# One layer of a hybrid SSD decoder: when weight sums are transferred, when u tiles are loaded, where the exponentials stand, and how many outputs share an accumulator

## The chip, the cores and the metric

The kernel runs on one core of a Trainium2 chip. The metric is the device time of one execution in microseconds, as the median of several runs. The engines are called PE (matmul), DVE, ACT, POOL and SP, as the profile calls them. Each takes its instructions in the order in which the program lists them. DMAs issued on POOL (software queue), SP and ACT (hardware queues) run on the same 16 DMA engines.

## What is computed

One layer of a decoder on 512 tokens and 16 learned leading tokens (528 columns), D = 1024, float32 in and out:

```python
u = rmsnorm(h, mix_norm_w)
proj = u @ w_in                                  # pool | z | xBC | dt | gates
gates = sigmoid(proj[..., OFF_GATE:] + b_gate)
y_pool = pool_mixer(u_pool, ...) @ w_pool_up     # causal means over 2, 4, 8, 16 tokens
xbc = silu(causal_depthwise_conv(xbc, conv_w, conv_b))
y = ssd_chunked(xs, softplus(dt_raw + dt_bias), -exp(a_log), B, C) + xs * d_skip
y = rmsnorm_per_group(y * silu(z)) * ssd_norm_w
h = h + (gate_pool * y_pool + gate_ssd * (y @ w_ssd_out)) @ w_o
h = h + relu(rmsnorm(h) @ w_ff1) ** 2 @ w_ff2
out = rmsnorm(h)[:, 16:]
```

The SSD part has 8 groups of 4 heads (head size 64, state 128) and runs in chunks of 128 tokens. Inside a chunk each head needs exp(a_cs[l] - a_cs[s]) below the diagonal, and exp(a_cs[l]) for what earlier chunks leave behind.

## The kernel before

Tiles have 128 partitions. A float32 operand is split into a rounded high part and the rest (`hi`, `lo`, type fp32r), and a product is three matmuls: hi x hi, hi x lo, lo x hi. A weight block (128 x 1024, 512 KB) is loaded by SP into `raw` (3 buffers), cast to `whi` by ACT (L95) and subtracted to `wlo` by DVE (L97); there are 4 buffers of each of the two.

The order of the work is made by a scheduler from the order in which the code lists it. `tc.issue_after(x)` puts what stands under it behind instruction x. Tile pools add the waits for buffers.

After a start (norm, dt, first group's projections, four gates) the program walks through the 8 groups (loop at L904). For group g, `weave` (L704) alternates the steps of these generators:

- `ssd(g)` (L569): POOL loads `abc`, the row a_cs broadcast to all partitions (L577, 1 MB, one buffer). PE transposes B and x (`ptb`, `ptm`, `ptx`). ACT makes exp(a_cs) in `eb` (L609), and the decay in `abc`: relu of the difference for two heads (L614; DVE does the other two, L617), then two exponentials (L620, L621). PE makes `pcb`, and DVE multiplies it into `abc` (L652, `masked`). PE makes the states (`pst`), the part of the earlier chunks (`po`) and of the own chunk (`py`, L667). DVE puts `yt` together (L670 to L674). ACT squares it (L679, `squared`), PE sums the squares (`png`, L685), ACT takes the root (L688), and ACT and DVE split the result (`yh`, `yl`).
- `group_proj(g + 1)` (L508): the next group's projections. B, C (and x up to group 3) are plain products (`px`, L197, L199) with a convolution (`conv`, L415: ACT L418, DVE L421, ACT's silu L423). From group 4 on, x's two tiles are made together by `pair` (L472) from seven products of sums of weights and sums of u (`pqx`, L485). Then z's two tiles (`pz`) and their silu (`zt`, L562), in some groups a gate ahead of them (`pgp`). In group 4 `out_half` (L800) comes first, in group 7 `out_part`.
- `sums_of_u` (L863) in groups 0 to 2: it loads u's tiles k and k + 4 from HBM into `ra` and `rb` (one buffer each), combines their halves on DVE (`combine`, L874), and splits the two results into the tiles `T` (`form`, L881; ACT and DVE). Group 0 does tile pair 0, group 1 does 1, group 2 does 2 and 3.
- `weight_sums_at` (L763): sums of weight blocks made by DMAs from HBM to HBM, on POOL's queue. A set takes 4 or 8 transfers, half of them with an add. Each transfer is tied to a small POOL copy (L770) of one column of `mark[0]`, the tile written last, so POOL waits for that tile; transfers are spread evenly over the steps of a group.

`out_half` (L800) makes 8 output blocks of 512 columns (`pso`) in 4 PSUM tiles of 1024 columns (`psum2`, two buffers), two blocks to a tile; ACT copies each block to SBUF (L806) and sends it to HBM.

The exponentials of `eb` (L608, L609) stand behind x's silu (`x_ready`) in groups 0 to 4 and behind z's silu (`z_ready`) in groups 5 to 7. ACT has its functions in tables: exponential, silu, sigmoid and root each need a table load (`ACT_TABLE_LOAD`) when another was used before.

The rest of the program (pool branch, merge, w_o, the MLP) follows the groups.

Of the kernel before, what the change touches and what calls it, by code (L numbers as in the profile page):

```python
# [12 lines left out]
ALU = mybir.AluOpType  # L13
# [42 lines left out]
SETS_POOL = 0  # L56

PLAIN = 4

# [5 lines left out]
def kernel(ctx: ExitStack, tc, xT, x, w, fx, f1, f2, vec, fnw, out):  # L65
# [125 lines left out]
    def proj(outs, wblk, rhs):  # L191

        for part in range(2):
            for k in range(NK):
                wt = wblk[part][:, k * P : (k + 1) * P]
                for o, c in outs:
                    pe.matmul(o, wt, rhs[0][k][:, c], start=part == 0 and k == 0, stop=part == 1 and k == NK - 1)  # L197
                    if part == 0:
                        mm[0] = pe.matmul(o, wt, rhs[1][k][:, c], start=False, stop=False)  # L199
# [10 lines left out]
    def narrow(ps):  # L210
        return [(ps, slice(NM, L))]
# [198 lines left out]


    mark = [None]
    x_ready, z_ready, filled = {}, {}, {}

    def conv(dst, src, ct):  # L415
        n = dst.shape[-1]
        e = src.shape[-1] - n
        act.activation(dst, src[:, e:], AF.Identity, bias=col(V_CB, ct), scale=col(V_CW, ct * 4 + 3))  # L418
        for j in range(1, 4):
            o = max(0, j - e)  # L420
            dve.scalar_tensor_tensor(dst[:, o:], src[:, e + o - j : e + n - j],  # L421
                                     col(V_CW, ct * 4 + 3 - j), dst[:, o:], op0=ALU.mult, op1=ALU.add)
        silu = act.activation(dst, dst, AF.Silu)  # L423
        mark[0] = dst[:, :1]
        if ct < 16:
            x_ready[ct // 2] = silu

    def group_tiles(g):
        xc = gc.tile([P, 2, L], F32, tag="xc", name=f"xc{g}")
# [42 lines left out]
    def pair(kind, g, r):  # L472

        ps = psum2(f"pq{kind}{g}")
        banks = (ps[:, :HALF], ps[:, 512 : 512 + HALF])
        operands = pair_operands(PAIRS.index((kind, g)))
        one, two = HF
        for m, f, n, start, stop in MULTIPLY:
            o = banks[n]
            wt = next(operands)  # L480
            f = factor_u(f)
            for low in range(2):
                for k in range(4):
                    wk = wt[low][:, k * P : (k + 1) * P]
                    pe.matmul(o, wk, f[k][0], start=start and not low and k == 0,  # L485
                              stop=stop and low == 1 and k == 3, skip_group_check=True)
# [21 lines left out]
    def group_proj(g, cur, gate=None):  # L508
# [60 lines left out]
    def ssd(g, cur):  # L569
# [35 lines left out]
        ap = abc.rearrange("p (i j) l -> p i j l", j=2)  # L605
        for j in range(2):
            js = slice(64 * j, 64 * j + 64)
            with tc.issue_after((z_ready if g in X_PAIRS[1:] else x_ready)[g].ins):  # L608
                act.activation(eb[js, :, :], ap[js, :, j, :], AF.Exp)  # L609
        dm = abc.rearrange("p r (c l) -> p r c l", c=4)  # L610
        for r in range(R):
# [92 lines left out]
    def weave(a, b, n, sums, side):  # L704

        end = object()
        a, sums = [a], [sums]
        while a or b or side:
            for t in [a] + [b] * n:
                for q in (t, sums):  # L710
                    if q and next(q[0], end) is end:
                        q.pop(0)
            side = [q for q in side if next(q, end) is not end]
        for q in sums:
            for _ in q:
                pass
# [23 lines left out]
            for t in sets for n in SUMS[t[0]]}  # L740

    def weight_steps():
        t = sets.pop(0)
        src = {"fx": fx, "f1": f1, "f2": f2}[t[0]][t[1]]
        o = {n: wsum[(*t, n)] for n in SUMS[t[0]]}
        put = nc.gpsimd.dma_start
        yield put(o["t1"], src[B11])
        yield put(o["s3"], src[B12])
        yield put(o["t1"], src[B12], accum_op=ALU.add)
        if "t2" in o:  # L750
            yield put(o["t2"], src[B22])
        yield put(o["s3"], src[B22], accum_op=ALU.add)
        if "t2" in o:
            yield put(o["t2"], o["t1"], accum_op=ALU.add)
            yield put(o["t4"], src[B21])
            yield put(o["t4"], o["t2"], accum_op=ALU.add)

    def weight_sums():
        for end in weight_steps():
            pass  # L760
        return end

    def weight_sums_at(n, pieces):  # L763
        total = sum(2 * len(SUMS[t[0]]) for t in sets[:n])
        steps = (e for _ in range(n) for e in weight_steps())
        put = i = 0
        while put < total:
            i += 1
            if put * pieces < i * total:
                at = pool.tensor_copy(seen, mark[0])  # L770
                with tc.issue_after(at.ins):
                    next(steps)
                put += 1
            yield
        assert next(steps, None) is None

    cur = group_tiles(0)
    for _ in group_proj(0, cur):
# [20 lines left out]

    def out_half():  # L800
        for dd in range(4):
            ps = psum2(f"pso{dd}")
            for i in range(2):
                ssd_out(2 * dd + i, ps[:, i * SEQ : (i + 1) * SEQ], range(8))
                o = staged(f"so{2 * dd + i}")
                act.copy(o, ps[:, i * SEQ : (i + 1) * SEQ])  # L806
                nc.scalar.dma_start(acc_d[2 * dd + i], o)
                mark[0] = o[:, :1]
                yield
# [50 lines left out]

    def sums_of_u(ks, g):  # L863

        one, two = HF

        def load(k):
            a, b = raw_pair("u", k)
            with tc.issue_after(abc_load[g].ins):
                for t, kk in ((a, k), (b, k + 4)):  # L870
                    nc.gpsimd.dma_start(t, u_d[kk])
            return a, b

        def combine(a, b, behind):  # L874
            with tc.issue_after(behind[g].ins):
                dve.tensor_tensor(b[:, two], a[:, two], b[:, two], op=ALU.subtract)
# [4 lines left out]
        def form(k, n, src, behind):  # L881
            hi, lo = T[n, "h", k], T[n, "l", k]
# [4 lines left out]
        t = load(ks[0])  # L887
        yield
        combine(*t, masked)
        yield  # L890
        form(ks[0], "0", t[0], y_first)
        if len(ks) > 1:
            form(ks[0], "1", t[1], y_first)
            t = load(ks[1])
        yield
        yield
        if len(ks) > 1:
            combine(*t, squared)
            form(ks[1], "0", t[0], squared)
            yield  # L900
        form(ks[-1], "1", t[1], squared)
        yield

    for g in range(G):  # L904
        nxt = group_tiles(g + 1) if g + 1 < G else None
        fill = [group_proj(g + 1, nxt, GATE_AT.get(g))] if nxt else [out_part()]
        if g == 4:
            fill = [out_half()] + fill
        weave(ssd(g, cur), fill, 2 if g == 4 else 1, weight_sums_at(SETS_AT[g], PIECES.get(g, 12)),
              [sums_of_u(SUMS_AT[g], g)] if g in SUMS_AT else [])  # L910
        cur = nxt
    gc_stack.close()
# [114 lines left out]

    for d in range(NK):
        t_load = nc.gpsimd.dma_start(acc[d], acc_d[d])
    for _ in range(SETS_POOL):  # L1030
        with tc.issue_after(t_load.ins):
            t_load = weight_sums()
    pend = [pooled_halves(*pool_tile(2 * POOL_ORDER[0] + i)) for i in range(2)]

    un = units()
# [782 lines left out]
```

## Time and profile before

| | us |
|---|---|
| median of 3 runs (1017.05 to 1018.7) | 1017.71 |
| the profiled execution | 1019.7 |
| its span, first to last instruction | 1018.0 |

The mean granted PE clock of the span is 0.996. A page of the profile gives, for one execution, the busy time of each engine and its share of the span, the span in slices, the DMA queues, the chain of work that ended last, and groups of equal instructions with their mean length and the idle time before them. Other views answer questions: a table by stretches of time, the list of who waited for whom, and the timeline of an engine. PEld is the weight load beside PE's matmuls. In a row of the timeline come start, length, engine, line, operation, output and inputs; the bracket at the end is the idle time just before it and what ended it.

### The profile page before, as it was taken

Reading aid. Unit: us, or ns where it says so; the run is one execution under the profiler, and the core shown is the slowest. Engines: PE = TensorE matmul, PEld = TensorE weight load, DVE = VectorE, ACT = ScalarE, POOL = GpSimd, SP = SyncE. Lnnn points to the kernel's source line nnn. Section 1 sums busy time; section 2 is a strip of 40 time slices with the busy share of each in tenths; the row PEclk is TensorE's granted clock in tenths of the full one; section 3 lists DMA queues with packets and bytes.
Section 4 is the critical chain, followed back from the end, with each engine's and each line's share of the span. In section 5 each row is a group of like instructions: output and inputs, shape, how many; then the busy total and the mean of one; then the engine's idle time right before and its main releaser. Section 6 shows DMA issues by size and latency. Waiting matters only on the chain.

```text
span 1018.0 us, 15702 instructions
## 1 busy us (share of the span) xinstructions
PE 998.0 (98%) x6047; PEld 876.6 (86%) x6047; DVE 799.0 (78%) x1153; ACT 603.6 (59%) x853; POOL 120.4 (12%) x215
## 2 busy tenths in 40 slices
PE   9999999999999999999999999999999999999997
PEld 7889888979788897987889888888889999999986
DVE  7968797778653787877689756877988888888885
ACT  8656769484833575665345533458656656665654
POOL 0001211212122212123400000221000000000000
PEclk9999999999999999999999999999999999999999
DMA  7265868566688748487933542879454554455432
GB/s 254 87 225 163 246 192 229 167 188 198 179 255 266 215 140 238 118 233 208 253 129 103 212 161 63 268 193 338 112 185 134 158 182 149 156 175 150 141 104 83
DMA packets 61803, 184.52 MB, mean 181 GB/s; under 512 B 7072, under 2 KB 8416, under 8 KB 60704
## 3 DMA queue, kind: packets, MB, share of 16 engines
q1 hardware_dynamic: 39456, 109.00, 32.3%
q0 software_dynamic: 18240, 67.51, 26.2%
q10 hardware_dynamic: 4032, 7.00, 1.9%
q8 instruction: 47, 0.77, 0.3%
q14 instruction: 28, 0.23, 0.1%
HBM read 173.13 MB, written 58.59 MB: 228 GB/s over the span
## 4 chain that ended last, share of the span: by engine, by line
PE 87%; ACT 6%; DMA 3%; DVE 2%; issue 1%; POOL 0%; ACTq 0%; DVEq 0%; POOLq 0%; SPq 0%
PE px L1437 8%; PE px L197 7%; PE alpha L1505 6%; PE px L1440 4%; PE px L199 4%; PE pz L197 4%; PE alpha L1508 3%; PE pgs L197 3%; PE pgp L197 2%; DMA raw<-in_w 2%; PE pqx L485 2%; PE py L667 2%; PE pz L199 2%; PE wo_alpha L1199 1%; PE pf L130 1%; PE pf L129 1%
## 5 line engine op out<-in xcount | busy, mean ns | idle before, releaser
L95 ACT CAST whi<-raw 128x1024 fp32r<-128x1024 f32 (+2 forms) x90 | 90.1, 1011 | 83.4 <-DMA raw<-in_w 18.1
L97 DVE TENSOR_TENSOR wlo<-raw,whi 128x1024 fp32r<-128x1024 f32 (+2 forms) x90 | 104.9, 1172 | 37.9 <-ACT whi L95 28.9
L197 PE MATMUL px<-uh,whi 128*128 128x264 f32 (+1 forms) x320 | 82.4, 295 | 0.0
L199 PE MATMUL px<-ul,whi 128*128 128x264 f32 (+1 forms) x320 | 79.9, 287 | 0.0
L1212 DVE TENSOR_TENSOR ht<-ht,alpha 128x1024 f32<-128x1024 f32 x35 | 42.7, 1219 | 29.1 <-PE alpha L1505 29.1
L197 PEld LDWEIGHTS px<-uh,whi 128*128 128x128 f32 x320 | 61.5, 192 | 1.3 <-issue 0.9
L199 PEld LDWEIGHTS px<-ul,whi 128*128 128x128 f32 x320 | 61.3, 192 | 0.3
L1135 ACT CAST shi<-rawf 128x1024 fp32r<-128x1024 f32 x42 | 44.2, 1053 | 28.7 <-PE alpha L1508 18.3
L1505 PE MATMUL alpha<-shi,hh 128*128 128x512 f32 x140 | 55.2, 394 | 0.0
L1508 PE MATMUL alpha<-shi,hl 128*128 128x512 f32 x140 | 54.7, 391 | 0.0
L1136 DVE TENSOR_TENSOR slo<-rawf,shi 128x1024 fp32r<-128x1024 f32 x42 | 51.2, 1218 | 0.6 <-ACT shi L1135 0.6
L1440 PE MATMUL px<-vsl,shi 128*128 128x256 f32 x192 | 47.4, 280 | 0.0
L1437 PE MATMUL px<-vsh,shi 128*128 128x256 f32 x192 | 47.4, 281 | 0.0
L197 PE MATMUL pz<-uh,whi 128*128 128x512 f32 x112 | 45.1, 402 | 1.5 <-ACT yh L697 1.3
L199 PE MATMUL pz<-ul,whi 128*128 128x512 f32 x112 | 44.6, 398 | 0.0
L197 PE MATMUL px<-uh,wlo 128*128 128x264 f32 (+1 forms) x320 | 42.5, 284 | 0.0
L197 PEld LDWEIGHTS px<-uh,wlo 128*128 128x128 f32 x320 | 40.1, 189 | 0.0
L1505 PE MATMUL alpha<-slo,hh 128*128 128x512 f32 x140 | 37.4, 389 | 0.0
L1437 PEld LDWEIGHTS px<-vsh,shi 128*128 128x128 f32 x192 | 36.2, 188 | 0.9
L1440 PEld LDWEIGHTS px<-vsl,shi 128*128 128x128 f32 x192 | 36.1, 188 | 0.9
L1440 PE MATMUL px<-vl,shi 128*128 128x256 f32 x144 | 36.1, 283 | 0.0
L1437 PE MATMUL px<-vh,shi 128*128 128x256 f32 x144 | 36.0, 282 | 0.0
(600 smaller groups left out, 3066.5 us busy)
## 6 DMA issues: line engine op xcount, KB each, us to landing
raw<-in_w SPq DMA_DIRECT2D x96, 512.0 KB, 4.9
f_t<-in_f POOLq DMA_DIRECT2D x38, 512.0 KB, 6.8
f_s<-in_f POOLq DMA_DIRECT2D x26, 512.0 KB, 7.4
b<-in_f SPq DMA_DIRECT2D x21, 512.0 KB, 4.6
rawf<-in_f SPq DMA_DIRECT2D x36, 256.0 KB, 3.0
rawf<-f_t SPq DMA_DIRECT2D x36, 256.0 KB, 2.9
abc<-acs_d POOLq DMA_DIRECT2D x8, 1024.0 KB, 7.6
f_t<-f_t POOLq DMA_DIRECT2D x12, 512.0 KB, 5.9
```

The source lines that it names most:

```text
L95: act.copy(hi[:, c], raw[:, c])
L97: dve.tensor_tensor(lo[:, c], raw[:, c], hi[:, c].bitcast(F32), op=ALU.subtract)
L197: pe.matmul(o, wt, rhs[0][k][:, c], start=part == 0 and k == 0, stop=part == 1 and k == NK - 1)
L199: mm[0] = pe.matmul(o, wt, rhs[1][k][:, c], start=False, stop=False)
L485: pe.matmul(o, wk, f[k][0], start=start and not low and k == 0, stop=stop and low == 1 and k == 3, skip_group_check=True)
L1135: splits.append((act.copy(hi, src), dve.tensor_tensor(lo, src, hi.bitcast(F32), op=ALU.subtract)))
L1136: dve.tensor_tensor(lo, src, hi.bitcast(F32), op=ALU.subtract)))
L1212: added[0] = dve.tensor_tensor(o, o, src, op=op)
L1437: pe.matmul(ps, m, f[k][0], start=start and not low and k == 0, stop=stop and low == 1 and k == 3, skip_group_check=True)
L1440: pe.matmul(ps, m, f[k][1], start=False, stop=False, skip_group_check=True)
L1505: pe.matmul(ps[t], hh[:, p, seg, st], m, start=bool(first and not low and p == 0), stop=bool(last and low and p == 1), skip_group_check=True)
L1508: pe.matmul(ps[t], hl[:, p, seg, st], m, start=False, stop=False, skip_group_check=True)
```

## The change

Five edits, in the groups alone:

- The transfers of the weight sums are given by a table (`SLOTS`): in a usual group five behind step 0, two behind step 2, one behind step 4, each bundle behind one POOL copy. Within a set (or two sets of four transfers) all plain transfers come first and the adds behind them. In `weave` the side work's step comes ahead of the sums' step.
- `sums_of_u` takes pairs 0 and 1 in group 0, 2 in group 1, 3 in group 2. A pair is asked for as soon as the pair before is split; pair 2 is so asked for in group 0, pair 3 in group 1.
- The exponentials of `eb` stand behind z's silu in all groups.
- z's products stand behind the pair's last product (`paired_up`) where there is a pair.
- Each output block of `out_half` has a PSUM tile of its own.

```diff
-SUMS_AT = {0: (0,), 1: (1,), 2: (2, 3)}
+SUMS_AT = {0: (0, 1), 1: (2,), 2: (3,)}
-SETS_AT = {0: 1, 1: 1, 2: 2, 3: 1, 4: 2, 5: 2, 6: 1, 7: 1}
-PIECES = {4: 21, 7: 14}
+SLOTS = {0: 5, 2: 2, 4: 1}
+SLOTS_LONG = {**SLOTS, 9: 4, 12: 2, 14: 2}
+SLOTS_LAST = {0: 2, 2: 2}
...
-            proj(narrow(ps), wt, X if first else U)
+            with tc.issue_after(paired_up[g].ins) if g in paired_up else nullcontext():
+                proj(narrow(ps), wt, X if first else U)
...
-            with tc.issue_after((z_ready if g in X_PAIRS[1:] else x_ready)[g].ins):
+            with tc.issue_after(z_ready[g].ins):
                 act.activation(eb[js, :, :], ap[js, :, j, :], AF.Exp)
...
-            for t in [a] + [b] * n:
-                for q in (t, sums):
-                    if q and next(q[0], end) is end:
-                        q.pop(0)
-            side = [q for q in side if next(q, end) is not end]
+            for i, t in enumerate([a] + [b] * n):
+                if t and next(t[0], end) is end:
+                    t.pop(0)
+                if i == 0:
+                    side = [q for q in side if next(q, end) is not end]
+                if sums and next(sums[0], end) is end:
+                    sums.pop(0)
...
+        for dst, src in q:
+            yield put(dst, src)
+        for dst, src in adds:
+            yield put(dst, src, accum_op=ALU.add)
...
+    def paced(slots):
+        for i in range(max(slots) + 1):
+            if i in slots:
                 at = pool.tensor_copy(seen, mark[0])
+                for _ in range(slots[i]):
+                    with tc.issue_after(at.ins):
+                        next(line)
             yield
...
         for dd in range(4):
-            ps = psum2(f"pso{dd}")
             for i in range(2):
-                ssd_out(2 * dd + i, ps[:, i * SEQ : (i + 1) * SEQ], range(8))
+                ps = psum2(f"pso{2 * dd + i}")[:, :SEQ]
+                ssd_out(2 * dd + i, ps, range(8))
...
+        if g == 0:
+            load(0)
         yield
-        combine(*t, masked)
+        combine(masked)
         yield
-        form(ks[0], "0", t[0], y_first)
-        if len(ks) > 1:
-            form(ks[0], "1", t[1], y_first)
-            t = load(ks[1])
+        form(ks[0], 0, y_first)
         yield
+        form(ks[0], 1, y_first)
+        if ks[0] < 3:
+            load(ks[0] + 1)
         yield
         if len(ks) > 1:
-            combine(*t, squared)
-            form(ks[1], "0", t[0], squared)
+            combine(squared)
             yield
-        form(ks[-1], "1", t[1], squared)
+            form(ks[1], 0, squared)
+            yield
+            form(ks[1], 1, squared)
+            load(ks[1] + 1)
         yield
```

More of the change, by code (lines that the diff above doesn't have):

```diff
@@ L484, in pair @@
                     wk = wt[low][:, k * P : (k + 1) * P]
-                    pe.matmul(o, wk, f[k][0], start=start and not low and k == 0,
-                              stop=stop and low == 1 and k == 3, skip_group_check=True)
+                    paired_up[g] = pe.matmul(o, wk, f[k][0], start=start and not low and k == 0,
+                                             stop=stop and low == 1 and k == 3, skip_group_check=True)
                     if not low:
@@ L742, in weight_steps @@
     def weight_steps():
-        t = sets.pop(0)
-        src = {"fx": fx, "f1": f1, "f2": f2}[t[0]][t[1]]
-        o = {n: wsum[(*t, n)] for n in SUMS[t[0]]}
+        ts = [sets.pop(0)]
+        if ts[0][0] == "f2" and sets and sets[0][0] == "f2":
+            ts.append(sets.pop(0))
         put = nc.gpsimd.dma_start
[L747 to L756, printed above, removed]
+        q, adds = [], []
+        for t in ts:
+            src = {"fx": fx, "f1": f1, "f2": f2}[t[0]][t[1]]
+            o = {n: wsum[(*t, n)] for n in SUMS[t[0]]}
+            q += [(o["t1"], src[B11]), (o["s3"], src[B12])]
+            adds += [(o["t1"], src[B12]), (o["s3"], src[B22])]
+            if "t2" in o:
+                q += [(o["t2"], src[B22]), (o["t4"], src[B21])]
+                adds += [(o["t2"], o["t1"]), (o["t4"], o["t2"])]
+        for dst, src in q:
+            yield put(dst, src)
+        for dst, src in adds:
+            yield put(dst, src, accum_op=ALU.add)
     def weight_sums():
@@ L761, in weight_sums @@
         return end
[L763 to L769, printed above, removed]
+    line = (e for _ in range(9) for e in weight_steps())
+    def paced(slots):
+        for i in range(max(slots) + 1):
+            if i in slots:
                 at = pool.tensor_copy(seen, mark[0])
-                with tc.issue_after(at.ins):
-                    next(steps)
-                put += 1
+                for _ in range(slots[i]):
+                    with tc.issue_after(at.ins):
+                        next(line)
             yield
-        assert next(steps, None) is None
     cur = group_tiles(0)
@@ L867, in load, with combine @@
         def load(k):
-            a, b = raw_pair("u", k)
+            raw = raw_pair("u", k)
             with tc.issue_after(abc_load[g].ins):
-                for t, kk in ((a, k), (b, k + 4)):
+                for t, kk in zip(raw, (k, k + 4)):
                     nc.gpsimd.dma_start(t, u_d[kk])
-            return a, b
-        def combine(a, b, behind):
+            u_raw.append(raw)
+        def combine(behind):
+            a, b = u_raw[-1]
             with tc.issue_after(behind[g].ins):
@@ L879, in combine, with form @@
                 dve.tensor_tensor(b[:, one], b[:, one], a[:, one], op=ALU.add)
-        def form(k, n, src, behind):
-            hi, lo = T[n, "h", k], T[n, "l", k]
+        def form(k, i, behind):
+            hi, lo = T["01"[i], "h", k], T["01"[i], "l", k]
+            src = u_raw[-1][i]
             with tc.issue_after(behind[g].ins):
@@ L908 @@
             fill = [out_half()] + fill
[L909 removed]
+        weave(ssd(g, cur), fill, 2 if g == 4 else 1, paced({4: SLOTS_LONG, 7: SLOTS_LAST}.get(g, SLOTS)),
               [sums_of_u(SUMS_AT[g], g)] if g in SUMS_AT else [])
@@ L1029 @@
         t_load = nc.gpsimd.dma_start(acc[d], acc_d[d])
-    for _ in range(SETS_POOL):
-        with tc.issue_after(t_load.ins):
-            t_load = weight_sums()
+    assert next(line, None) is None
     pend = [pooled_halves(*pool_tile(2 * POOL_ORDER[0] + i)) for i in range(2)]
```

11 lines of the change are left out of this document (4 added, 7 removed).

## The prediction

> **What bounds the kernel now.** I read the engine table first, then the chain of work that ended last, then busy time by stage, then the waits of TensorE (PE).
>
> ```profile
> PE 998.0 (98%) x6047; PEld 876.6 (86%) x6047; DVE 799.0 (78%) x1153; ACT 603.6 (59%) x853; POOL 120.4 (12%) x215
> ...
> PE 87%; ACT 6%; DMA 3%; DVE 2%; issue 1%; POOL 0%; ACTq 0%; DVEq 0%; POOLq 0%; SPq 0%
> ```
>
> PE is busy 998.0 of 1018.0 us and carries 87% of the chain. The matmuls that the change leaves are the same in number and size, so the time can fall only by PE's idle time, or by a clock that is not halved. The stages (columns: length, then PE, PEld, DVE, ACT and POOL busy with counts, PE clock, DMA share, GB/s) show where that lies:
>
> ```profile
> 115.00:160.00 45.00, 42.80 (x318) 39.53 (x318) 38.83 (x62) 33.59 (x45) 8.17 (x16) 1.00 0.74 208
> 160.00:209.00 49.00, 46.74 (x329) 42.19 (x328) 40.41 (x67) 31.90 (x43) 8.93 (x20) 0.98 0.65 186
> ...
> 265.00:357.00 92.00, 88.16 (x509) 75.50 (x509) 55.04 (x77) 48.85 (x67) 21.28 (x37) 1.00 0.80 227
> ...
> 404.00:440.00 36.00, 35.17 (x263) 33.10 (x264) 30.76 (x52) 21.80 (x34) 6.72 (x12) 0.95 0.62 176
> ...
> 496.00:1018.00 522.00, 516.53 (x2928) 453.78 (x2926) 417.70 (x549) 289.66 (x415) 25.77 (x42) 1.00 0.52 163
> ```
>
> The groups, the only place where the order changes, run from 72 to 496; PE idles there in patches (45.00 less 42.80 is 2.2 us in one, 3.8 in another). The last 522 us keep their order and are costed at nothing. In 404 to 440 the mean clock is 0.95: 0.05 x 36 is 1.8 us lost. Who made PE wait (total, times, longest):
>
> ```profile
> PE pso L129 <- ACT so L806: 2.5, 1, 2.5
> PE png L685 <- ACT qhg L311: 2.2, 2, 1.8
> PE ptx L597 <- DVE xddm L590: 1.8, 2, 1.5
> ...
> PE py L667 <- issue: 1.5, 1, 1.5
> PE pz L197 <- ACT yh L697: 1.3, 1, 1.3
> ```
>
> They are single events, seen in the timeline (start, length, engine, line, operation, and in brackets the idle time before):
>
> ```profile
> 133.24 0.99 PE L667 MATMUL py<-abc,xdt 128*64 128x128 f32 x14 [1.50 <-issue]
> 205.97 0.50 PE L685 MATMUL png<-qhg,ones_r 128*128 128x512 f32 x1 [1.77 <-ACT qhg L311]
> 208.45 0.63 PE L197 MATMUL pz<-uh,whi 128*128 128x512 f32 x1
> 211.16 0.39 PE L199 MATMUL pz<-ul,whi 128*128 128x512 f32 x1
> 280.31 0.50 PE L129 MATMUL pso<-yh,whi 128*128 128x512 f32 x1 [2.55 <-ACT so L806]
> 404.83 0.66 PE L597 MATMUL ptx<-ident,xc 128*128 128x128 f32 x4 [1.53 <-DVE xddm L590]
> ```
>
> After the idle patch at 206 a 512-column matmul takes 0.63 us in place of 0.39: the clock is halved for a while there too, as in the stage from 404. I price each halving at the 1.8 us above.
>
> **The change, part by part.**
>
> *An accumulator per output block.* Two outputs share a PSUM tile, and the second output's first matmul stands 2.55 us for the copy of the first, which is queued on ACT behind the exponentials. With a tile each, the second starts at once, and the third needs the copy only a block (24 matmuls) later. Gain 2.55.
>
> *u tiles one stage ahead.* In group 2 two tiles are loaded and the second pair is wanted in the same group:
>
> ```profile
> 193.36 0.70 POOL L871 DMA_DIRECT2D rbu<-u_d  x1
> 201.42 0.43 DVE L876 TENSOR_TENSOR rbu<-rau,rbu 128x264 f32<-128x264 f32 x1 [4.03 <-DMA rbu<-u_d]
> 203.85 0.76 DVE L421 SCALAR_TENSOR_TENSOR xc<-px,vs,xc 128x527 f32<-128x527 f32 x1
> 205.95 0.69 DVE L312 TENSOR_TENSOR qlg<-sqg,qhg 128x512 fp32r<-128x512 f32 x1
> 209.05 1.22 DVE L97 TENSOR_TENSOR wlo<-raw,whi 128x1024 fp32r<-128x1024 f32 x1
> ```
>
> DVE stands 4.03 us before it combines the pair, and qhg, png and z's products come late behind it: 1.77 plus about 0.5 in two smaller gaps, plus a halved clock. In the changed kernel groups 1 and 2 have one pair each, asked for a group earlier: gain 2.25 + 1.8.
>
> But group 0 now takes two pairs, and the second can't be asked for ahead, since the first holds its buffers. On POOL it stands behind the load of group 1's abc and behind two accumulating transfers, the second waiting until the first has landed. Rows for that:
>
> ```profile
> 97.56 0.57 POOL L577 DMA_DIRECT2D abc<-acs_d  x1 [1.41 <-PE py L667]
> 106.15 0.68 DVE L674 TENSOR_TENSOR yt<-yt,zt 128x512 f32<-128x512 f32 x1
> 112.18 1.98 PE L197 MATMUL pz<-uh,wlo 128*128 128x512 f32 x8
> ...
> fx_t<-fx_t POOLq DMA_DIRECT2D x4, 512.0 KB, 6.6
> ...
> rau<-u_d POOLq DMA_DIRECT2D x4, 264.0 KB, 8.1
> ```
>
> The first accumulation goes out shortly before abc, at about 95, and lands 6.6 us later, at 101.6; the second takes its place on the queue, and the tiles go out at about 103 and land 8.1 us later, at 111. DVE, done with y at about 105 to 106.8, stands some 5 to 6 us. Queued behind the waiting combine are two convolution steps, the group's sum of squares, its low half and the combine's next step, then the low half of z's second weight block: 0.43 + 0.76 + 0.69 + 0.76 + 0.69 + 0.43 + 1.22 = 5.0 us, so that block is ready at 116, and PE wants it at 112.18. I take 3.8 us of idle PE and one more halved clock, 1.8. Bounds: nothing if the pair lands by 107.2; 5.5 + 1.8 if it lands 1.7 later than I think. A gain is excluded, since PE doesn't wait there now.
>
> *Exponentials behind z's silu.* ACT in group 1 now:
>
> ```profile
> 114.12 1.05 ACT L95 CAST whi<-raw 128x1024 fp32r<-128x1024 f32 x1 [1.01 <-DMA raw<-in_w]
> 115.18 1.28 ACT L609 ACT_TABLE_LOAD   x1
> 116.48 1.06 ACT L609 ACTIVATE eb<-abc 64x1024 f32<-64x1024 f32 x1
> 117.55 1.28 ACT L562 ACT_TABLE_LOAD   x1
> 118.85 1.03 ACT L562 ACTIVATE zt<-pz 128x1024 f32<-128x1024 f32 x1
> ```
>
> One exponential runs ahead of silu, so its table is loaded, dropped and loaded again. The new order does silu first: two loads of 1.28 go from this group, and four of 45 in all. The exponentials end some 2.5 us earlier and py, which stood 1.50 at 133.24, doesn't wait: gain 1.5. Elsewhere the exponentials start later after z (by silu and its load, up to 2.3 us), which PE's projections ahead of py cover:
>
> ```profile
> 172.01 1.93 PE px L197 x16
> ...
> 180.39 1.93 PE px L197 x16
> ```
>
> These are the last passes of the two projections between z and py in group 2, 8.4 us apart, and py comes after both. If that cover were gone, it would cost 2.3 us a group. The Trainium skill, "ScalarE: Activation LUTs", section What ACT_TABLE_LOAD costs, gives about 1283 ns for the load and a drain of about 1380 more. By that, four loads would be 10.6 us of ACT and not 5.1; the rows show 1.28 and no drain (the cast ends at 115.17, the load starts at 115.18), so the trace agrees with the first half only.
>
> *z's products held behind the pair's products.* PE is in order, and z's matmuls among the pair's make it stand 1.3 us for z's operands. Held back, they are late for nobody but silu: gain 1.3, bounds 0 and, if the pair's operands now find PE with nothing to fill, a loss of the same size.
>
> *Sums at the beginning of the group.* The bytes are the same, in fewer POOL steps (42 fewer rows of copies and issues). At the group's end there is less to share with the last weight blocks, and the square root comes ahead of x's silu, so ptx at 404.83 should find its buffer free: gain 1.53 + 1.8. The bursts' cost is the slow rival below; here I take nothing, as weight loads have blocks in hand.
>
> **Sum.** Gains 2.55 + 2.25 + 1.5 + 1.3 + 1.53 = 9.1, and two halved clocks, 3.6: 12.7. Against them 3.8 + 1.8 = 5.6 in group 0. A static order that removes waits brings others that can't be seen from here: DVE and ACT are next in line (38.83 and 33.59 of 45). I charge a quarter of the 9.1, 2.3. Net 12.7 - 5.6 - 2.3 = 4.8 us. The profiled execution took 1019.7 with its span of 1018.0; it should become 1013.2 of span and 1014.9. The runs' median is 1017.71, 2.0 below that execution: predicted 1012.9.
>
> **Rivals.**
> 1. *Nothing stands in group 0.* The pair lands by 107.2 and nothing new waits: 1017.7 - 12.7 = 1005.0. For: the tiles' transfers are short. Against: 4.03 us at the same place in group 2.
> 2. *Given back.* Each removed wait turns into one on DVE, so that beside the 5.6 all of the rest, 7.1, goes too: 1017.7. For: DVE is busy 86% from 115 to 160. Against: the waits named are of one operation each, and not of DVE's load.
> 3. *Slower: bursts starve the weights.* Each group begins with four transfers of 512 KB at once, while PE needs a weight block every 5.6 us (from 57.44 to 63.02 below, two blocks' last passes). Rows:
>
> ```profile
> raw<-in_w SPq DMA_DIRECT2D x96, 512.0 KB, 4.9
> ...
> ACT whi L95 <- DMA raw<-in_w: 18.1, 10, 5.1
> 249.17 9.17 DMA raw<-in_w
> ...
> 57.44 2.09 PE pgp L197 x9
> 63.02 2.10 PE pgp L197 x9
> ```
>
> A block lands in 4.9 us, but took 9.17 when abc and two transfers ran: 4.3 late. If the blocks in hand cover half, 2.1 us in each of seven groups is 15, and the time 1017.7 - 12.7 + 5.6 + 15 = 1025.6. It decides from (12.7 - 5.6) / 7, 1.0 us a group. For: ACT already waits 18.1 us for weights. Against: none of PE's waits above is for them. The Trainium skill, "DMA: Bandwidth & Descriptors", section Queues, rings and completion order, says that each engine goes round between its queues packet by packet; by that rule a burst halves the weights' rate while it lasts, which is this rival.
>
> That the change doesn't do what it says holds for group 0's second pair, and is in the forecast.
>
> **How the numbers follow.** Forecast 0.50 (1009 to 1015.6), rival 1 0.16, rival 2 0.12, rival 3 0.22. A measurement of this kernel tells about 0.2%, 2 us. Faster: 0.50 + 0.16 = 0.66; the same: 0.12; slower: 0.22. The range goes from rival 1's time, 1004.5, to 1023, which leaves out the upper half of rival 3.
>
> **What would show it.** Right: no wait of pso for so, none of py in group 1, PE idle near 112 to 116 behind DVE's combine for a u tile, no halved clock near 207 and 405, 41 table loads. Wrong: PE waits on casts that wait for raw weights early in the groups (rival 3), or the combine in group 0 without a wait (rival 1).

## The result, and the profile after

| | us | ratio to before (95% interval) |
|---|---|---|
| before, median of 7 runs (1014.89 to 1019.77) | 1017.05 | |
| after, median of 7 runs (1021.49 to 1028.14) | 1025.53 | 1.0068 (1.0039 to 1.0096) |
| profiled execution after | 1024.82 (span 1023.1) | |

The kernel became slower by 0.7%, some 7 us by the ratio (the medians lie 8.5 apart); I had forecast 1012.9 and given 1023 as the upper end. The engine table and the chain's shares by engine, first page:

```profile
PE 997.6 (98%) x6047; PEld 879.1 (86%) x6047; DVE 800.3 (78%) x1153; ACT 598.5 (58%) x849; POOL 102.1 (10%) x173
...
PE 89%; DMA 3%; DVE 3%; ACT 3%; issue 1%; POOL 0%; ACTq 0%; DVEq 0%; SPq 0%; POOLq 0%
```

PE's busy time is that of before (997.6 against 998.0), and so is the number of its matmuls. The span is 5.1 longer, so the loss is idle PE. The stages (same columns as before):

```profile
115.00:160.00 45.00, 41.04 (x312) 38.13 (x312) 40.87 (x66) 28.84 (x40) 8.84 (x16) 1.00 0.76 223
160.00:209.00 49.00, 48.07 (x330) 43.87 (x331) 40.77 (x64) 31.77 (x44) 9.11 (x12) 0.97 0.69 196
...
404.00:440.00 36.00, 34.88 (x261) 31.92 (x259) 32.73 (x52) 23.75 (x36) 5.25 (x11) 1.00 0.65 183
```

The halved clock of 404 to 440 is gone (0.95 to 1.00), and 115 to 160 now idles 4.0 us in place of 2.2. What PE waited for (total, times, longest):

```profile
PE pz L197 <- ACT rax L501: 3.1, 1, 3.1
PE pz L197 <- ACT gp L730: 2.9, 1, 2.9
PE pqx L483 <- ACT rbx L494: 2.8, 3, 0.9
PE pz L197 <- DVE wlo L97: 2.4, 1, 2.4
PE ptx L596 <- DVE xddm L589: 1.9, 1, 1.9
PE pqx L483 <- DVE rbx L497: 1.6, 3, 0.6
...
PE pqx L483 <- DVE rax L490: 1.5, 1, 1.5
PE pqx L483 <- DVE rbx L499: 0.5, 1, 0.5
PE pqx L483 <- ACT rbx L492: 0.5, 1, 0.5
```

None of the waits that I wanted gone is left: pso for so, png, py, pz for yh. Two families have come. The first are the five pqx rows, 2.8 + 1.6 + 1.5 + 0.5 + 0.5 = 6.9 us. Timeline of PE in after, at the pair of x in group 5's projections:

```profile
343.99 0.39 PE L483 MATMUL pqx<-t0h,whip 128*128 128x264 f32 x1 [1.51 <-DVE rax L490]
...
346.19 0.39 PE L483 MATMUL pqx<-t1h,whip 128*128 128x264 f32 x1 [0.48 <-ACT rbx L492]
...
348.86 0.39 PE L483 MATMUL pqx<-t0h,whip 128*128 128x264 f32 x1 [0.93 <-ACT rbx L494]
```

A pair's seven products go by turns into two PSUM banks, and each starts only when ACT or DVE has taken the earlier product out of its bank. The same place in before:

```profile
340.41 0.47 PE L197 MATMUL pz<-uh,whi 128*128 128x512 f32 x1 [1.26 <-ACT yh L697]
...
340.95 0.28 PE L485 MATMUL pqx<-t0h,whip 128*128 128x264 f32 x1
...
342.42 0.39 PE L197 MATMUL pz<-uh,whi 128*128 128x512 f32 x1
```

There z's matmuls stood between the products and filled those gaps; their one wait of 1.26 was the price. The second family stands at the ends of groups 0, 1 and 3. First DVE and PE in group 0 of after, then ACT, PE, SP and POOL at the end of group 1, and ACT and PE at the end of group 3:

```profile
110.32 0.43 DVE L880 TENSOR_TENSOR rbu<-rau,rbu 128x264 f32<-128x264 f32 x1 [4.97 <-DMA rbu<-u_d]
114.94 2.12 PE L197 MATMUL pz<-uh,wlo 128*128 128x512 f32 x8 [2.38 <-DVE wlo L97]
121.41 0.66 PE L596 MATMUL ptx<-ident,xc 128*128 128x128 f32 x4 [1.93 <-DVE xddm L589]
```

```profile
148.00 0.82 POOL L760 DMA_DIRECT2D fx_t<-fx_t  x1 [2.84 <-DMA fx_t<-fx_t]
148.54 0.85 POOL L576 DMA_DIRECT2D abc<-acs_d  x1
149.74 0.57 POOL L874 DMA_DIRECT2D rbu<-u_d  x1 [0.36 <-issue]
150.99 0.33 SPq L87 DMA_DIRECT2D raw<-in_w  x1
157.80 1.04 ACT L95 CAST whi<-raw 128x1024 fp32r<-128x1024 f32 x1 [2.79 <-DMA raw<-in_w]
160.93 0.62 PE L197 MATMUL pz<-uh,whi 128*128 128x512 f32 x1 [2.86 <-ACT gp L730]
...
260.62 1.04 ACT L95 CAST whi<-raw 128x1024 fp32r<-128x1024 f32 x1 [1.71 <-DMA raw<-in_w]
261.57 0.37 ACT L501 COPY rax<-pqx 128x264 f32<-128x264 f32 x1
262.00 0.50 PE L197 MATMUL pz<-uh,whi 128*128 128x512 f32 x1 [3.12 <-ACT rax L501]
```

Read the second fence downwards: POOL issues a sum's add (512 KB), abc (1 MB) and a u tile (264 KB) within 2.3 us; the weight block asked for at 150.99 is cast 6.8 us later; what frees pz's PSUM tile stands behind that cast on its engine, and PE waits. At 262 the chain is the same, with the copy of a pair's product behind a cast that waits 1.71 for its weights.

### The profile page after: what moved, and what is told of

Read it like the earlier page. It is cut to its first block, busy times and chain, and to the rows that moved or that the text cites. A ratio compares the mean times of both kernels' runs of the same rounds, so it can differ in the third digit from the quotient of the medians.

```text
span 1023.1 us, 15629 instructions
## 1 busy us (share of the span) xinstructions
PE 997.6 (98%) x6047; PEld 879.1 (86%) x6047; DVE 800.3 (78%) x1153; ACT 598.5 (58%) x849; POOL 102.1 (10%) x173
## 4 chain that ended last, share of the span: by engine, by line
PE 89%; DMA 3%; DVE 3%; ACT 3%; issue 1%; POOL 0%; ACTq 0%; DVEq 0%; SPq 0%; POOLq 0%
PE px L1443 8%; PE alpha L1511 6%; PE px L197 6%; PE pz L197 5%; PE px L1446 4%; PE alpha L1514 3%; PE px L199 3%; PE pgs L197 3%; PE pz L199 3%; PE pqx L483 2%; PE pgp L197 2%; DMA raw<-in_w 2%; PE py L666 1%; PE pso L129 1%; PE wo_alpha L1205 1%; PE pf L130 1%
```

## The experiments

The theories at the start: PAIR (z's products held back took PE's filler away), BURST (the sums' bytes, in bursts, delay the weights), FIRST PAIR (group 0's second u pair in front of DVE). Three came later: ORDER (the place of the casts in their engines' queues is the cause, whatever the bytes), LATE EXP (the exponentials, kept back until z's silu, are what costs beside the bursts) and COLLISION (the late exponentials bring weights and u tiles into one stretch with the sums and abc). Every ratio below is to the kernel before, run on the same chip; where two ratios are subtracted, they can come from two chips. A profile is one execution.

### One part undone or alone

**e1**, the change without `paired_up`:

```diff
-            with tc.issue_after(paired_up[g].ins) if g in paired_up else nullcontext():
-                proj(narrow(ps), wt, X if first else U)
+            proj(narrow(ps), wt, X if first else U)
```

> The changed kernel with one part undone: z's products are no longer held behind the pair's last product. Theory PAIR (z's products had filled PE while the pair's one PSUM bank was copied out, and the changed kernel waits there for about 8.7 us in groups 4 to 6): those waits shrink to under 2 us, and the time falls by 6 to 9 us, to 1017 to 1019. Rival BURST (the sums' transfers in bursts keep ScalarE's weight casts waiting, and pz behind them): at most 2 us fall, 1023.5 or more, and the two pz waits near 161 and 262 us stay at 3 us each. Rival FIRST PAIR (group 0's second u pair in front of DVE): no change, 1025.

Measured: 1.0018 (0.9996 to 1.0040). Waits of PE:

```profile
PE pz L197 <- ACT gp L729: 3.1, 1, 3.1
PE pz L197 <- ACT rax L501: 3.1, 1, 3.1
PE pz L197 <- DVE wlo L97: 1.7, 1, 1.7
...
PE pz L197 <- ACT yh L695: 1.3, 1, 1.3
```

All pqx rows are gone, the 1.3 for yh is back, the other waits stay. PAIR holds for 1.0068 - 1.0018 = 0.0050, 5.1 us; 5.6 follows from the rows (6.9 less 1.3), or 4.4 with a wait of psp of 1.2 that is back as well.

**e2**, the kernel before with these lines alone:

```diff
+            with tc.issue_after(paired_up[g].ins) if g in paired_up else nullcontext():
+                proj(narrow(ps), wt, X if first else U)
```

> The kernel before with one part added: z's products behind the pair's last product, nothing else. PAIR: waits of pqx of 5 to 9 us appear in groups 4 to 6 and the time rises by 5 to 9 us, to 1022 to 1026. BURST and FIRST PAIR: within 2 us of 1017.

Measured: 1.0056 (1.0029 to 1.0084). Waits of PE, the first rows:

```profile
PE pqx L485 <- ACT rbx L496: 2.8, 3, 0.9
PE ptx L598 <- DVE xddm L591: 2.4, 1, 2.4
PE pqx L485 <- DVE rbx L499: 1.6, 3, 0.6
```

The same pqx rows to a tenth. PAIR is shown from both sides, and is most but not all of the loss.

This profile warns of something else, too. Up to 340 us the compute engines take their instructions in the order of before, and yet PE doesn't wait for py near 133 or for pso near 280 (1.50 and 2.55 in before), and ptx near 119 waits 2.38 (0.22 in before). Single waits of one profile come and go from one execution to another in the same order.

**e3**, the change with `sums_of_u`, its table and the order inside `weave` as before:

```diff
-SUMS_AT = {0: (0, 1), 1: (2,), 2: (3,)}
+SUMS_AT = {0: (0,), 1: (1,), 2: (2, 3)}
...
```

> The changed kernel with the u tiles as before: one pair in group 0, one in 1, two in 2, each loaded in its own stage. FIRST PAIR (the second pair's difference in front of weights on DVE, 2.5 + 2.1 us of waits in group 0): those two go, but the waits of group 2 on the u tiles, 2.25 and a halved clock of 1.8, return; the sum is a fall of 0 to 2 us, 1023.5 to 1025.5. If FIRST PAIR is the whole cause: 1018. PAIR and BURST: 1025 within 2.

Measured: 1.0072 (1.0045 to 1.0100). The waits of group 0 went, and others of 2.6 (png near 158), 2.7 (pz near 211) and 1.8 (po near 92) came. FIRST PAIR is not the cause.

**e4**, the change with `weight_steps` and the pacing of the sums as before:

```diff
-SLOTS = {0: 5, 2: 2, 4: 1}
+SETS_AT = {0: 1, 1: 1, 2: 2, 3: 1, 4: 2, 5: 2, 6: 1, 7: 1}
+PIECES = {4: 21, 7: 14}
...
```

> The changed kernel with the weight sums paced and ordered as before (12 to 21 pieces spread over a group, one POOL copy ahead of each). BURST: the pz waits near 161 and 262 us (3.1 and 3.3) go with the halved clock behind them (1.7 each), a fall of 6 to 10 us, to 1016 to 1019, less 1.5 for the ptx wait of before that may return. PAIR: the pqx waits stay at 8 us, a fall of at most 3 us, 1022.5 or more.

Measured: 1.0020 (0.9998 to 1.0042): all three waits of pz went, the pqx rows and ptx's 1.9 stayed, and a wait of po for DVE of 3.8 in four pieces came. Inside the change the bursts cost 0.0048.

**e5**, e1 and e4 together:

```diff
-            with tc.issue_after(paired_up[g].ins) if g in paired_up else nullcontext():
...
-SLOTS = {0: 5, 2: 2, 4: 1}
+SETS_AT = {0: 1, 1: 1, 2: 2, 3: 1, 4: 2, 5: 2, 6: 1, 7: 1}
...
```

> The changed kernel with two parts undone: z's products free again, and the weight sums paced and ordered as before. What stays of the change: accumulator per block, exponentials behind z's silu, u tiles a stage ahead. If the two parts cost what each gave when undone alone (ratios 1.0068 to 1.0018 and to 1.0020, so 0.0050 and 0.0048) and add up: ratio 0.997, 1014 us where the kernel before takes 1017. If both undo the same waits by a shift of the static order: ratio 1.000 to 1.002. If the parts that stay are worth the 6 us that their waits measured before: 0.994.

Measured: 0.9978 (0.9958 to 0.9998). The two add up. What stays of the change is worth 2 us, not the 6 of its waits.

**e6**, before with accumulator and exponentials alone:

```diff
-            with tc.issue_after((z_ready if g in X_PAIRS[1:] else x_ready)[g].ins):
+            with tc.issue_after(z_ready[g].ins):
...
-            ps = psum2(f"pso{dd}")
...
+                ps = psum2(f"pso{2 * dd + i}")[:, :SEQ]
```

> The kernel before with two parts of the change alone: an accumulator per output block, and all exponentials behind z's silu. By the waits of before (pso for so 2.55, py 1.5): the two waits go and the time falls by 4 us, ratio 0.996, if nothing else comes late. By the other reading (each edit moves the static order, and new waits of 2 us or more come up wherever it moves): the two waits go, others of 2 to 6 us in sum appear in groups 1 to 4, ratio 0.998 to 1.003.

Measured: 0.9995 (0.9977 to 1.0013). The waits of pso and py went, and two of pz came, 3.2 near 206 and 2.2 near 259. With the sums spread as before, then, late exponentials and accumulators together change nothing that the runs can tell.

### The bytes

**e7**, the change with narrow sums: each transfer moves 64 columns in place of 1024. The sums are left out of what is computed, since the loads that would read them (here and in the MLP) read a block of the input of the same size. PE, ACT, DVE and POOL have exactly the order of the changed kernel:

```diff
-            yield put(dst, src)
+            yield put(dst[:, few], src[:, few])          # few = slice(0, 64)
...
-                src = fx[s, q[m]] if m in q else wsum["fx", s, m]
+                src = fx[s, q[m]] if m in q else fx[s, B11]
...
```

> The changed kernel with the same instructions in the same order on PE, ACT and DVE, and as many transfers of sums at the same places, each 64 columns wide instead of 1024; the loads that would read the sums read a block of the same size from the input instead, so the sums are left out of what is computed. BURST (the bytes of the sums in a burst delay the weights): the waits of pz near 114, 161 and 262 us and of ptx near 121 (2.4, 2.9, 3.1, 1.9) shrink to under a quarter, and the time falls by 8 us or more, to 1017 or less. ORDER (the place of the casts and subtractions in the queues of ACT and DVE makes the weights' buffers come free late, and their latency is the usual one): the four waits stay above two thirds of their size, the weights' transfers land in 6 us as before, and the time falls by less than 3 us.

Measured: 0.9931 (0.9903 to 0.9958). ACT at the place of the cast of 157.80, and the waits of pz that are left:

```profile
150.31 1.05 ACT L95 CAST whi<-raw 128x1024 fp32r<-128x1024 f32 x1
```

```profile
PE pz L197 <- DVE xc L421: 0.5, 1, 0.5
PE pz L197 <- ACT rax L501: 0.4, 1, 0.4
```

The cast that stood 2.79 for its weights doesn't stand, and of the four waits of 2.4, 2.9, 3.1 and 1.9 two are left, of 0.5 and 0.4. The weight block behind that cast landed in 4.0 us in place of 6.8. ORDER falls: the queues are the same, only bytes were taken away. (In the changed kernel no load on SP waits for a sum's transfer in the groups, so it isn't that wait that went.) The bytes cost the changed kernel 1.0068 - 0.9931 = 0.0137.

**e8**, before with the bursts alone:

```diff
-SETS_AT = {0: 1, 1: 1, 2: 2, 3: 1, 4: 2, 5: 2, 6: 1, 7: 1}
+SLOTS = {0: 5, 2: 2, 4: 1}
...
+        for dst, src in q:
+            yield put(dst, src)
+        for dst, src in adds:
+            yield put(dst, src, accum_op=ALU.add)
```

> The kernel before with one part added: the weight sums in bursts at a group's start, plain transfers first, as the changed kernel has them. If they alone cost what undoing them gave (0.0048): ratio 1.005, 1022 us, with waits of pz or ptx near the ends of groups 0 to 3. If they cost only together with the u tiles a stage ahead (both on POOL's queue): ratio 0.999 to 1.002. By the prediction's own terms (the waits of ptx near 404 and the halved clock go): 0.997.

Measured: 0.9923 (0.9896 to 0.9951), 1011.8 us, against all three expectations. The waits of pso (2.5) and png (2.2) are gone and that of ptx has shrunk from 1.8 to 0.6, though accumulator and u tiles are as before, and PE, ACT and DVE keep the order of before through all the groups but for one DMA issue on ACT; a wait of po of 1.7 near 92 came. BURST, as it stood, falls: bursts by themselves gain 7.8 us.

### What the bursts collide with

**e9**, the change with the exponentials as before (here and in e6 and e10 the exponentials are moved by this condition alone):

```diff
-            with tc.issue_after(z_ready[g].ins):
+            with tc.issue_after((z_ready if g in X_PAIRS[1:] else x_ready)[g].ins):
```

> The changed kernel with one part undone: the exponentials of groups 0 to 4 may again start behind x's silu. The sums' bursts alone gave 0.9923 and the changed kernel with z's products free 1.0018, so accumulator, exponentials and u tiles cost 0.0095 on top of the bursts. Theory LATE EXP (the exponentials and the eight Relu behind them, kept back until z's silu, stand in front of weight casts on ACT at the group's start, while the bursts delay the weights): the waits of pz near 161 and 262 go, ratio 0.996 to 0.999 (only z's products held back, 0.005, remain of the loss). Rival U TILES (the u tiles a stage ahead are what collides with the bursts): ratio 1.004 to 1.007, the waits of pz stay above 2 us each.

Measured: 0.9995 (0.9975 to 1.0015), just above the range of LATE EXP and well under that of its rival. The waits near 161 and 262 are gone; the one of pz for wlo near 115 is still there, 3.0 in place of 2.4.

**e10**, before with bursts and late exponentials:

```diff
+SLOTS = {0: 5, 2: 2, 4: 1}
...
+            with tc.issue_after(z_ready[g].ins):
```

> The kernel before with two parts: the sums in bursts and the exponentials behind z's silu. LATE EXP: the exponentials undo what the bursts gain (0.9923), ratio 0.999 to 1.003. U TILES: 0.991 to 0.994, as with the bursts alone.

Measured: 1.0012 (0.9989 to 1.0036). The exponentials alone undo the whole gain of e8. ACT and DVE of e10:

```profile
156.93 1.04 ACT L95 CAST whi<-raw 128x1024 fp32r<-128x1024 f32 x1 [4.46 <-DMA raw<-in_w]
...
208.65 1.04 ACT L95 CAST whi<-raw 128x1024 fp32r<-128x1024 f32 x1 [3.40 <-DMA raw<-in_w]
```

```profile
208.85 0.43 DVE L874 TENSOR_TENSOR rbu<-rau,rbu 128x264 f32<-128x264 f32 x1 [4.02 <-DMA rbu<-u_d]
```

In e8 the rows at the first two places and at the combine are:

```profile
155.06 1.05 ACT L95 CAST whi<-raw 128x1024 fp32r<-128x1024 f32 x1 [0.52 <-DMA raw<-in_w]
...
204.30 1.05 ACT L95 CAST whi<-raw 128x1024 fp32r<-128x1024 f32 x1
```

```profile
199.95 0.43 DVE L876 TENSOR_TENSOR rbu<-rau,rbu 128x264 f32<-128x264 f32 x1 [1.35 <-DMA rbu<-u_d]
```

With the exponentials late, the weights of the last blocks come 3.40 to 4.46 us after ACT is ready for them; without, 0.52 or in time. What is issued ahead of the block cast at 208.65, and the block itself, from POOL and SP of e10:

```profile
196.41 0.57 POOL L575 DMA_DIRECT2D abc<-acs_d  x1 [4.23 <-DVE yt L672]
...
197.44 0.82 POOL L757 DMA_DIRECT2D f_s<-in_f  x1
198.01 0.83 POOL L869 DMA_DIRECT2D rau<-u_d  x1
199.05 0.57 POOL L869 DMA_DIRECT2D rbu<-u_d  x1 [0.20 <-issue]
200.58 0.33 SPq L87 DMA_DIRECT2D raw<-in_w  x1
```

In e8 the first of these two u tiles goes out at 191.19, 6.8 us earlier.

**e11**, the change without `paired_up` and with the exponentials as before (the edits of e1 and e9):

```diff
-            with tc.issue_after(paired_up[g].ins) if g in paired_up else nullcontext():
-            with tc.issue_after(z_ready[g].ins):
+            with tc.issue_after((z_ready if g in X_PAIRS[1:] else x_ready)[g].ins):
```

> The changed kernel with two parts undone: z's products free, and the exponentials as before. Kept are the accumulator per block, the u tiles a stage ahead and the sums in bursts. LATE EXP: the loss is gone, ratio 0.990 to 0.993, 1010 us. U TILES: 1.000 to 1.003.

Measured: 0.9939 (0.9918 to 0.9960): the loss is gone, if not quite to the 0.990 to 0.993 expected.

**e12**, before with bursts and accumulators:

```diff
+SLOTS = {0: 5, 2: 2, 4: 1}
...
+                ps = psum2(f"pso{2 * dd + i}")[:, :SEQ]
```

> The kernel before with the sums in bursts and an accumulator per output block. The wait of pso for so (2.55 before) had gone already with the bursts alone, so the accumulator should add nothing: ratio 0.990 to 0.995, the same as 0.9923. If the accumulator is what costs beside the bursts: 0.998 or more.

Measured: 0.9919 (0.9897 to 0.9942), 1012.2 us. This and e8 beat both kernels. The kernels now make a ladder, each with one part more:

| sums in bursts | + accumulators | + u tiles ahead | + z held back | + late exponentials |
|---|---|---|---|---|
| e8 0.9923 | e12 0.9919 | e11 0.9939 | e9 0.9995 | after 1.0068 |
| -0.0077 | -0.0004 | +0.0020 | +0.0056 | +0.0073 |

The steps of the accumulators and the u tiles lie inside the intervals. The step of the u tiles takes in the order inside `weave`.

**e13, e14, e15**: before, e8 and e10 with the narrow sums of e7, which again leave the sums out of the result (the lines of e13; the loads change as in e7):

```diff
+        put = lambda d, v, **k: nc.gpsimd.dma_start(d[:, few], v[:, few], **k)
```

> The kernel before with its sums' transfers 64 columns wide, as in e7 (the sums left out, the loads reading a block of the input instead; the same order of instructions but for a stretch around the start of group 4). It gives what the bytes of the sums cost before the change. If BURST holds of the change alone (bursts collide, spread sums did not): ratio 0.997 to 1.000. If the spread sums collided just as much: 0.985 to 0.993, like the 0.9931 of the changed kernel, whose pair waits of 0.005 are in that.

> The kernel before with the sums in bursts, and these 64 columns wide (the sums left out, as in e13). If the bursts at the group's start have hardly any cost in bytes left (as the 0.9923 with full sums would have it): ratio 0.988 to 0.992. If the bursts still cost as much by their bytes as they do in the changed kernel (0.0137): 0.980 or less.

> The kernel before with the sums in bursts and the exponentials behind z's silu, sums 64 columns wide (left out, as in e13); PE, ACT and DVE have the order of e10. COLLISION (the later exponentials cost 0.0089 because the weights and u tiles come into one stretch with the sums and the load of abc): without the sums' bytes the cost goes, the ratio is within 0.003 of e14. ORDER (the exponentials cost by their place on ACT, whatever the transfers): 0.007 to 0.010 above e14, and the waits of png near 158 and of pz near 210 stay at 2 us or more.

| kernel | full sums | narrow sums | cost of the bytes |
|---|---|---|---|
| before (e13) | 1 | 0.9899 (0.9872 to 0.9925) | 0.0101 |
| bursts (e8, e14) | 0.9923 | 0.9897 (0.9870 to 0.9923) | 0.0026 |
| bursts and late exponentials (e10, e15) | 1.0012 | 0.9890 (0.9864 to 0.9917) | 0.0122 |
| the whole change (e7) | 1.0068 | 0.9931 (0.9903 to 0.9958) | 0.0137 |

The 0.0026 of the bursts lies inside the intervals. e15 keeps the order of e10 on PE and DVE to the last instruction, and on ACT and POOL but for one DMA issue each; e13 and e14 have another order than before and e8, above all between 190 and 260 us.

This settles the main point. With narrow sums the late exponentials cost nothing (0.9897 to 0.9890); with full sums they cost 0.0089. It is COLLISION. The casts of e15 at the two places of e10:

```profile
150.80 1.06 ACT L95 CAST whi<-raw 128x1024 fp32r<-128x1024 f32 x1 [1.37 <-PE pgp L199]
...
199.64 1.05 ACT L95 CAST whi<-raw 128x1024 fp32r<-128x1024 f32 x1 [0.51 <-DMA raw<-in_w]
```

The weight block of the second cast landed in 8.0 us in e10, in 5.1 in e15, where abc and the u tiles go out just as close ahead of it and only the sum is narrow, and in 5.5 in e8. And the kernel before had paid for the same bytes all along; the waits of PE in e13:

```profile
...
PE py L667 <- issue: 1.5, 1, 1.5
PE pz L197 <- ACT yh L697: 1.3, 1, 1.3
...
PE ptx L597 <- DVE xddm L590: 0.2, 1, 0.2
```

pso and png are gone and ptx is down from 1.8 to 0.2: these had come from the sums' bytes (e8, in the order of before, has no pso and no png either). yh stays to the tenth. py is 1.5 here, but 0.7 in e14 and nothing in e2, so of py this tells nothing.

**e16**, e10 with abc's load behind the u tiles:

```diff
+        with tc.issue_after(u_last[g - 1].ins) if g - 1 in u_last else nullcontext():
+            abc_load[g] = nc.gpsimd.dma_start(abc, acs_d[hs, :].partition_broadcast(P))
```

> The kernel of e10 (sums in bursts, exponentials behind z's silu) with one transfer moved: the load of group 3's abc (1 MB) comes behind the second u pair of group 2 on POOL's queue, where the kernel with the bursts alone has it, instead of two steps ahead of it. PE, ACT and DVE keep the order of e10. COLLISION at that place: POOL no longer stands 4.2 us for abc's buffer ahead of the u tiles, they land before 204 and not at 208.9, the wait of pz near 210 (2.8) and the halved clock there (0.03 of 56, 1.7) go, and the ratio falls by 0.004 from 1.0012 to 0.995 to 0.999; the wait of png near 158 (2.9), whose transfers are not moved, stays. If the place of that one transfer doesn't matter: the wait near 210 stays above 2 us, ratio 1.000 to 1.003.

Measured: 1.0013 (0.9989 to 1.0036), no change. The wait of pz near 210 shrank from 2.8 to 1.0, and the next one, png near 213, came with 2.6. ACT there:

```profile
210.57 1.04 ACT L95 CAST whi<-raw 128x1024 fp32r<-128x1024 f32 x1 [4.46 <-DMA raw<-in_w]
```

The weights are as late as in e10, and the u tiles, which were to land before 204, are combined at 207.89. So the forecast of COLLISION for this place was missed. But the edit only brought abc nearer to that weight block: abc goes out at 196.41 in e10 and at 200.47 here, the block is asked for at 200.58 and 201.44, and it landed in 9.1 us after 8.0. So e16 doesn't show what abc further from that block would give.

## Why the prediction was wrong, step by step

The forecast summed to -4.8 us (4.8 faster); the ladder sums to 0.0068, +6.9 us.

- **Exponentials behind z's silu: gain 1.5 forecast, 7 to 9 us lost** (0.0073 on top of the rest, 0.0089 on the bursts alone). This is the step that failed most. What it said of ACT was right, 41 table loads. py doesn't wait near 133, as it said, but it doesn't in e2, e9 and e11 either, where the exponentials stand as before. Without the sums' bytes the step does no harm (e15), nor, beside the accumulators, with the sums spread as before (e6): the loss belongs to the late exponentials and the bursts together, and the sum priced each by itself. What failed was "PE's projections ahead of py cover": I looked for the cost on the path from the exponentials to py. The edit shifts the static order of all engines, and in the new order the last weight blocks of groups 1 to 3 and the u tiles are in transfer together with sums and abc.
- **z's products held back: gain 1.3 forecast, 5.1 to 5.7 lost** (e1, e2). The mechanism stood in the text, "PE with nothing to fill", with a bound that was unfounded: a loss "of the same size". The bound had to come from the seven products of a pair, which wait for their two banks in three groups: 6.9 us, 4.0 of it in the first of them.
- **Sums at the beginning of the group: 1.53 + 1.8 = 3.3 forecast; alone they gain 7.8** (e8). The reason, less to share with the last weight blocks at a group's end, is borne out by the bytes' cost, 0.0101 to 0.0026. The size was off since two of the waits that they remove were booked elsewhere.
- **Accumulators: gain 2.55 forecast, -0.0004 measured beside the bursts.** The copy that freed the tile was late, and the bursts alone removed that; a second tile adds nothing then. The evidence is e8 and e12, since e13 has another order from 190 us on; and in e2 pso doesn't wait with the tile and the order of before, so 2.55 was the wait of one execution.
- **u tiles: 4.05 gained and 5.6 lost forecast, a net loss of 1.55; +0.0020 (2 us) measured, not distinct from nothing.** Group 0 came out as described: the pair lands at 110.3 (forecast 111), DVE stands 4.97 ("5 to 6"), PE 2.4 and, further on, 1.9, without a halved clock (1.00 in 115 to 160). With the narrow sums both waits of PE go (e7). The gain near 206 was again that of the sums' bytes: png doesn't wait in e8, with the old u tiles and in the order of before.
- **The charge of 2.3 for a new order** was a quarter of the gains. The waits of pz at 161 and 262 alone are 6.0 and each is followed by a halved clock. (The range's lower end, 1004.5, is called rival 1's time, which the sum gives as 1005.0; nothing hangs on it.)
- **Rival 3 named the time (1025.6) by luck, and half of the cause.** Weights are starved, as it said, but not early in the groups by bursts of four transfers: these gain by themselves, so its 15 us never came. It happens at the groups' ends, with the late exponentials; and 5 of the 7 us have no transfer in them. The packet-by-packet turns between queues that the prediction cited from the Trainium skill, "DMA: Bandwidth & Descriptors", section Queues, rings and completion order, would make bytes on POOL's queue delay SP's weights; e7 agrees in the direction (0.0137 for bytes alone), and no run here shows the turns themselves.

Open: how the weights lose to the sums at a group's end, and what abc and the u tiles add. e16 moved one of these and left it close ahead of the weights; narrowing abc or the u tiles was not tried.

## What to carry to other kernels

When several small waits stand on different engines, ask whether one shared resource stands behind them: the same instructions with a sixteenth of the bytes told more than the waits' names, and showed that three gains, booked for three edits, were one. Before booking a single wait as a gain, look for it in a second profile of the same order: py's and pso's were not there (e2). An edit that moves a group of instructions under a static order also moves transfers: price it by what will be on the DMA engines together, not only by the path from the moved instruction to its reader. And before holding back work that "makes PE wait", look at what that work fills: here it covered 6.9 us of waits for PSUM and cost 1.3.

## What was not expected of the hardware

- The median of the weights' transfers tells little. Over 100 to 265 us a 512 KB block landed in 6.5 us (median of 22) in before and in 4.9 in after, which is slower.
- Contention shows in the spread, too: on one chip the kernel before ran from 1013.16 to 1020.71 (10 runs), and with narrow sums from 1006.41 to 1007.09 (6 runs). With full sums in bursts (e8, another chip) it was 1010.43 to 1012.13 (6 runs), against 1013.21 to 1024.83 of before there (23 runs).
- PE's clock was halved at 160.93, after 2.86 us of idle PE, for eight matmuls at 0.62 to 0.63 us; after 2.38 idle at 114.94 it was not. The length of one idle stretch doesn't decide alone, though: in before 1.53 us at 404.83 were followed by matmuls of 264 columns at 0.42 in place of 0.28 us (the stage's clock is 0.95). The Trainium skill, "TensorE: Matmul & The Clock Gate", Part 1, gives an idle window of about 3.4 us; here less than that was enough.
